# A hybrid decoder step: earlier splitting of the first merged sums, side work let out by chunk length, first x tile on another queue

## The chip, the core and the metric

The kernel runs on one core of a Trainium2 chip. A core has a matrix engine (TensorE, PE in the profile; its weight loads are shown as PEld), VectorE (DVE), ScalarE (ACT), GpSimd (POOL) and SyncE (SP), which work through their own instruction queues in order and wait for each other by semaphores. Data moves between the device memory and the core's memory (SBUF) by DMAs, which here are issued by SyncE and, at the end, by ScalarE. TensorE writes to eight PSUM banks. The metric is the device time of one execution, in microseconds; lower is better.

## The reference

One layer of a decoder trunk in float32, for 256 prompt tokens and 8 sample tokens (264 columns, N), model width 2048:

```
xn = rms_norm(x, g_mix);  z = xn @ w_in          # pool u | lru x | lru gelu gate | conv a | conv b
y_pool = pool_mixer(u) @ w_pool_br               # window means minus token, 4 groups, per-group map w_pool_grp
y_lru  = (rg_lru(causal_dwconv(lru_x)) * gelu(gate)) @ w_lru_br
y_conf = silu(layer_norm(causal_dwconv(a * sigmoid(b), 31 taps))) @ w_conf_br
gates  = sigmoid(xn @ w_gate + b_gate)           # three gates of width 2048
x = x + (g_a * y_pool + g_b * y_lru + g_c * y_conf) @ w_out
x = x + square(relu(rms_norm(x, g_mlp) @ w_up)) @ w_down      # inner width 8192
y = rms_norm(x, g_final)
```

The new states of the pooling, the two convolutions and the LRU are outputs too.

## The kernel before, in words

**Products in three parts.** A float32 product is made from three products of rounded parts: each operand is split into a high part (rounded to the matrix engine's fp32r format) and a low part (the rest). For each weight tile and k tile, `mm3` (L283) issues high x high, low weight x high input, high weight x low input, all through `mm` (L281), with a 128x128 weight tile and 264 columns.

**The weight stream.** All weights come as one list of chunks (`weight_plan`, L97). A dense chunk is two k tiles by 512 columns, so 2 x 4 x 3 = 24 matmuls. Four lru chunks and one grp chunk hold 128x128 blocks, 12 matmuls each, and one chunk, none, is empty and only keeps the pairs even. There are 472 dense chunks, 478 in all. Each pair is loaded to `raw` (6 chunks deep, `dma_pair`, L222) by SyncE. `split(j)` (L258) makes its high part in `whi` on ScalarE (L264) and its low part in `wlo` on VectorE (L265); both have four buffers, so chunk j can be split once TensorE has finished chunk j - 4.

Chunk numbers that matter, before the change: 0 to 15 are w_in for the lru x; 28 to 31 end w_in's pooling and first gelu-gate groups; 32 to 43 the second gelu-gate group with the lru chunks at 34, 37, 40 and 42; 44 to 59 the two conf groups of w_in; 60 to 69 the first gate group, with grp at 64 and none at 65; 86 starts the pooling branch projection, 87 the LRU branch projection; 182 to 189 are w_conf_br (group 0 ends at 184, 1 at 185, 2 at 188, 3 at 189); 190 starts w_out.

**The loop.** For chunk i the program writes, in this order: `split(i + 3)` (L1013), DMA issues, the chunk's matmuls, at a group's end the evacuation of its four PSUM tiles (mostly VectorE), and then `run_bg()` (L308), which lets out side work. The engines' queues hold the instructions in that order. There is no other scheduler: the place of an instruction in its engine's queue is set by the chunk in which it was written.

**Side work.** The branches between the projections (convolutions, LRU gates and scan, gelu, pooling, the conf branch) are lists of small operations in three queues, lru, pool and conf, in this order of preference. Each stage names an engine, a cost in microseconds, and how many chunks the next stage waits (`stage`, L296). Each engine has a credit; every `run_bg` adds an income (1.8 for ScalarE, 1.5 for VectorE, 2.4 for GpSimd; 1.3 and 1.0 once the flag lru is set), with at most half an income carried over, and lets out operations while the credit covers them. Work that is not queued is charged with `spend`. Other work is put off by a fixed number of chunks with `later` (L305). A flag such as pool, lru or conf (`mark`, L302) is set when all before it in the queue has been let out; the program asserts it before a chunk that reads the result. The pooling is: four running sums on GpSimd, four `diff` (L783, VectorE), a split in high and low parts (`stage_split`, L544), then `grp_mm` (L801) in the grp chunk, whose result is evacuated by ScalarE (L806) and split again. `lru_tail` (L568) holds tanh (L578), decay (L581, with another table), root, products and scan (L603) of the LRU. `lru_gate_mm` (L550) issues an lru chunk, its two sigmoids on ScalarE and, one chunk later, a product on VectorE (L562).

**The merged sums.** `branch_evac` (L840) multiplies a branch projection by its gate (L844). For the third branch it adds the partial sum of the other two on GpSimd (L850) and puts off the split for w_out: high part three chunks later on ScalarE (L856), low part five chunks later on VectorE (L860). The first w_out chunks, 190 to 193, read the four sums of group 0, chunk 194 on those of group 1.

**The start.** `dma_head` (L250) issues three loads on SyncE: norm weights with the first x tile and the first half weight chunk (396 KB), a second x tile with its half chunk, and the two other halves. Seventeen warm-up matmuls on constants (L376) come first on TensorE. The first x tile is made into its parts by VectorE (L394, L203), the first weights by ScalarE (L274).

Of the kernel before, what the change touches and what calls it, by code (L numbers as in the profile page):

```python
# [19 lines left out]
N = TP + TS  # L20
KD = D // P
# [35 lines left out]
HEAD = N + 512  # L57
FIRST = 16
CH = 1024
NRAW = 6  # L60
NHI = 4
LRU_AT = (1, 3, 5, 6)
GRP_AT = 3
WARM = 17
LEAD = 4
SINGLE = 16
# [30 lines left out]
def weight_plan():  # L97

    def gate(t):
        return ("w_gate", 0, 16, t)

    def w_in(m):
        return ("w_in", 0, 16, m)

    def branches(g):
        return [("w_pool_br", 0, 4, g), ("w_lru_br", 0, 8, g)]

    walks = [[w_in(1), w_in(2)], [w_in(0), w_in(3)], [w_in(4)], [w_in(6), w_in(5)], [gate(0)], [gate(4), gate(1)]]  # L110
    walks += [branches(0), [gate(5), gate(2)], branches(1), [gate(6), gate(3)], branches(2), [gate(7)], branches(3)]
    walks += [[gate(8 + g)] for g in range(4)]
    walks += [[("w_conf_br", 0, 4, g + i) for i in range(2)] for g in (0, 2)]
    walks += [[("w_out", 0, 16, m + i) for i in range(2)] for m in (0, 2)]
    for q in range(4):
        up = [("w_up", 0, 16, q * 4 + m) for m in range(4)]
        walks += [up[:2], up[2:]] if q else [up[:1], up[1:2], up[2:]]
        walks += [[("w_down", q * 16, 16, m + i) for i in range(2)] for m in (0, 2)]

    groups, chunks, at = [], [], 0  # L120
    for walk in walks:
        mine = range(len(groups), len(groups) + len(walk))
        groups += walk
        todo = {}
        for gi in mine:
            for c in range(groups[gi][2] // 2):
                todo.setdefault(slot_of(("dense", gi, c), groups), []).append((gi, c))
        places = sorted(todo, reverse=abs(max(todo) - at) < abs(min(todo) - at))
        order = []
        for place in places:  # L130
            todo[place].sort(key=lambda x: (x[1], x[0]) if mine[0] == 0 and place != places[-1] else x)
            order += todo[place]
        at = places[-1]
        for gi, c in order:
            own = [o for o in order if o[0] == gi]
            n = own.index((gi, c))
            chunks.append(("dense", gi, c, CH, n == 0, n == len(own) - 1))
            if groups[gi] == w_in(4) and n in LRU_AT:
                chunks.append(("lru", LRU_AT.index(n), 0, 512))
            if groups[gi] == gate(0) and n == GRP_AT:  # L140
                chunks += [("grp", 0, 0, 512), ("none", 0, 0, 0)]
    return groups, chunks
# [3 lines left out]
def hybrid_step(ctx: ExitStack, tc: tile.TileContext, first, par_in, st_in, wall, y_out, st_out):  # L146
    nc = tc.nc
# [4 lines left out]
    def f(ap):  # L152
        return ap.bitcast(F32)
# [26 lines left out]
    def both(t, slot, row, rows):  # L180
        out = []
        for r in (row, row + rows):
            at = SKEW + r * ROW + slot * OCT
            out.append(bass.AP(tensor=t.tensor, offset=t[:, at:].offset,
                               ap=[list(t.ap[0]), [HOP, N // (STRETCH * OCT)], [STEP, STRETCH], [1, OCT]]))
        return tuple(out)
# [4 lines left out]
    def in_sum(k):  # L191
        return both(a_all, 3 - k // 4, k % 4, 4)
# [4 lines left out]
    def v(t):  # L197
        return t.rearrange("p (a b c) -> p a b c", b=STRETCH, c=OCT)
# [17 lines left out]
    done = set()  # L216


    groups, chunks = weight_plan()
# [18 lines left out]
    head = [b_all[i] for i in (1, 2)]  # L238
# [9 lines left out]
        return head[0][:, KD + c * HEAD + N:KD + c * HEAD + HEAD]  # L248

    def dma_head():  # L250
        for t, a, b, o in ((0, 0, KD + HEAD, 0), (0, KD + HEAD, KD + 2 * HEAD, 0), (1, 0, CH, KD + 2 * HEAD)):
            nc.sync.dma_start(head[t][:, a:b], first[:, o + a:o + b])

    def dma_x(j):
# [31 lines left out]

    queues = {"lru": [], "pool": [], "conf": []}
    ready_at = dict.fromkeys(queues, 0)  # L290
    credit = {"act": 0.0, "dve": 0.0, "pool": 0.0}
    income = {"act": 1.8, "dve": 1.5, "pool": 2.4}
    now = [0]
# [11 lines left out]
    def later(n, fn):  # L305
        delayed.append((now[0] + n, fn))

    def run_bg():  # L308
        if "lru" in done:
            income.update(act=1.3, dve=1.0)  # L310
        for item in [d for d in delayed if d[0] <= now[0]]:
            delayed.remove(item)
            item[1]()
        for e in credit:
            credit[e] = min(credit[e], 0.5 * income[e]) + income[e]
        for q, todo in queues.items():
            while todo and ready_at[q] <= now[0]:
                if isinstance(todo[0], str):
                    if todo[0] not in done:
                        break  # L320
                    todo.pop(0)
                    continue
                eng, cost, fns, gap = todo[0]
                if eng != "none" and credit[eng] < min(cost, income[eng]):
                    break
                fns.pop(0)()
                if eng != "none":
                    credit[eng] -= cost
                if not fns:
                    todo.pop(0)  # L330
                    ready_at[q] = now[0] + gap

    def spend(**kw):
        for e, c in kw.items():
            credit[e] -= c
# [31 lines left out]


    dma_head()
    nc.vector.memset(ones, 1.0 / D)  # L370
    nc.vector.memset(eps, EPS)
# [446 lines left out]
    def gate_tile(br, g, m):  # L818
        if br == 2:
            return G[:, 4 * g + m, :]  # L820
        if br and g % 2:
            return GEL[:, m, :]
        return G[:, g % 2 * 8 + br * 4 + m, :]

    def partial(k):
        return (TM if k < 8 else RA)[:, k % 8, :]
# [13 lines left out]
    def branch_evac(br, g, m, ps):  # L840
        assert "grp" in done and (br < 1 or "lru" in done) and (br < 2 or "conf" in done)
        t = gate_tile(br, g, m)
        k = g * 4 + m
        nc.vector.tensor_tensor(t, ps[:, :N], t, op=ALU.mult)  # L844
        spend(dve=0.43)
        if br == 1:
            nc.gpsimd.tensor_tensor(partial(k), t, gate_tile(0, g, m), op=ALU.add)
            spend(pool=0.8)
        if br == 2:
            nc.gpsimd.tensor_tensor(t, t, partial(k), op=ALU.add)  # L850
            spend(pool=0.8)
            later_split(*in_sum(k), t, 3, 2)

    def later_split(hi, lo, x, n, gap):
        def one():
            nc.scalar.copy(hi, v(x))  # L856
            spend(act=0.4)

        def other():
            nc.vector.tensor_tensor(lo, v(x), f(hi), op=ALU.subtract)  # L860
            spend(dve=0.35)

        later(n, one)
        later(n + gap, other)
# [75 lines left out]
    def group(gi):  # L940
        name, k0, _, m = groups[gi]
        if name == "w_in":
            def rhs(i):
                return in_a(i)
            fn = {0: pool_evac, 1: lru_x_copy, 2: lambda c, p: lru_x_evac(4 + c, p), 3: gel_evac,
                  4: lambda c, p: gel_evac(4 + c, p), 5: ca_evac, 6: cb_evac}[m]
            return rhs, fn
        if name == "w_gate":
            return in_a, (lambda c, p: gate_evac(m // 4, m % 4, c, p))
        if name == "w_pool_br":  # L950
            assert "grp" in done
            return (lambda i: in_half(Q(), i)), (lambda c, p: branch_evac(0, m, c, p))
        if name == "w_lru_br":
            assert "lru" in done
            return (lambda i: in_half(LH(), i)), (lambda c, p: branch_evac(1, m, c, p))
        if name == "w_conf_br":
            assert "conf" in done
            return (lambda i: in_half(Q(), 4 + i)), (lambda c, p: branch_evac(2, m, c, p))
        if name == "w_out":
            return in_sum, (lambda c, p: out_evac(m * 4 + c, p))  # L960
        if name == "w_up":
            return bpart, (lambda c, p: up_evac(m // 4, (m % 4) * 4 + c, p))
        q = k0 // 16
        return (lambda i: hid(q, i)), (lambda c, p: down_evac(q, m * 4 + c, p))
# [43 lines left out]
    for i, ch in enumerate(chunks):  # L1008
# [69 lines left out]
        if i == 14:  # L1078
            later(0, x_rms)
        run_bg()  # L1080
    while delayed:
        now[0] += 1
        run_bg()
# [143 lines left out]
```

## Time and profile before

| what | value |
|---|---|
| median of 3 runs | 1314.7 us (1314.19 to 1316.95) |
| the profiled execution | 1315.07 us |
| its span in the trace | 1313.3 us |
| TensorE busy | 1300.7 us (99%) |
| VectorE busy | 839.9 us (64%) |
| ScalarE busy | 719.9 us (55%) |
| GpSimd busy | 98.3 us (7%) |
| bytes moved | 257.21 MB, mean 196 GB/s |

The profile shows one execution. Its own time is 1.8 us above its span, for what lies around the first and last instruction. A line of a timeline has the start and the length in microseconds, the engine, the line of the kernel, the operation, the tiles (written <- read), the shapes and the number of like instructions in a row; in square brackets stands how long the engine idled before it and what ended that. The kernel's helpers record many operations under one line, so that the tiles tell them apart. wlo and whi are the parts of the weights, A holds the parts of xn and later of the merged sums.

### The profile page before, as it was taken

How to read it: one execution, taken by the hardware profiler on the slowest of the kernel's cores; microseconds unless marked ns; L12 is line 12 of the kernel's file. 1: busy time of each engine (PE TensorE's matmuls, PEld its weight loads, DVE VectorE, ACT ScalarE, POOL GpSimd, SP SyncE). 2: the span in 40 equal slices, each digit the busy share in tenths (PEclk: the TensorE clock that was granted, in tenths of full speed). 3: DMA queues.
4: the chain of work that ended last, by engine and by line, in shares of the span. 5: the costliest groups of instructions: out<-in, count | busy, mean ns of one | idle time of the engine just before them, and what ended most of it. 6: DMA issues, size and time to landing. Idle time of an engine off the chain costs nothing.

```text
span 1313.3 us, 26597 instructions
## 1 busy us (share of the span) xinstructions
PE 1300.7 (99%) x11421; PEld 1298.1 (99%) x11421; DVE 839.9 (64%) x1126; ACT 719.9 (55%) x1034; POOL 98.3 (7%) x125
## 2 busy tenths in 40 slices
PE   9999999999999999999999999999999999999997
PEld 9999999999999999999999999999999999999996
DVE  8787898777776758577655554565446644564554
ACT  7667687676764645456545334553335533354454
POOL 0320020101012104012000000000000000000022
PEclk9999999999999999999999999999999999999998
DMA  9555556555565555555655555555555555555552
GB/s 347 210 185 186 184 200 218 195 192 196 194 224 194 189 197 184 198 193 169 218 193 193 194 193 193 195 194 192 194 194 194 194 196 194 194 198 194 194 196 77
DMA packets 40565, 257.21 MB, mean 196 GB/s; under 512 B 4480, under 2 KB 6528, under 8 KB 11520
## 3 DMA queue, kind: packets, MB, share of 16 engines
q1 hardware_dynamic: 40016, 254.92, 55.9%
q8 instruction: 89, 1.46, 0.4%
q10 hardware_dynamic: 432, 0.61, 0.1%
q14 instruction: 28, 0.23, 0.1%
HBM read 252.30 MB, written 3.21 MB: 195 GB/s over the span
## 4 chain that ended last, share of the span: by engine, by line
PE 97%; DVE 1%; ACT 1%; issue 0%; DVEq 0%; ACTq 0%
PE acc L281 97%; ACT whi L264 0%; DVE wlo L265 0%; PE acc L376 0%; DVE y L1115 0%; ACT tmp L578 0%; DVE tmp L628 0%; DVE G L844 0%; ACT L581 0%; DVE A L860 0%; ACT tmp L581 0%; DVE G L562 0%; DVE acc L1106 0%; DVEq L1204 0%; DVE G L1105 0%
## 5 line engine op out<-in xcount | busy, mean ns | idle before, releaser
L265 DVE TENSOR_TENSOR wlo<-raw,whi 128x1024 fp32r<-128x1024 f32 (+1 forms) x478 | 586.5, 1230 | 452.4 <-ACT whi L264 447.4
L264 ACT CAST whi<-raw 128x1024 fp32r<-128x1024 f32 (+1 forms) x478 | 493.6, 1036 | 534.4 <-PE acc L281 500.9
L281 PE MATMUL acc<-A,whi 128*128 128x264 f32 x3968 | 676.9, 274 | 2.0 <-DVE A L860 2.0
L281 PEld LDWEIGHTS acc<-A,whi 128*128 128x128 f32 x3968 | 597.1, 188 | 2.7 <-DVE A L860 2.2
L281 PE MATMUL acc<-A,wlo 128*128 128x264 f32 x1984 | 540.6, 274 | 0.3
L281 PEld LDWEIGHTS acc<-A,wlo 128*128 128x128 f32 x1984 | 370.1, 187 | 0.9 <-DVE wlo L265 0.9
L281 PE MATMUL acc<-xn,whi 128*128 128x264 f32 x2048 | 349.3, 274 | 0.0
L281 PEld LDWEIGHTS acc<-xn,whi 128*128 128x128 f32 x2048 | 308.3, 187 | 0.0
L281 PE MATMUL acc<-xn,wlo 128*128 128x264 f32 x1024 | 280.7, 274 | 0.0
L281 PEld LDWEIGHTS acc<-xn,wlo 128*128 128x128 f32 x1024 | 191.8, 187 | 0.0
L281 PE MATMUL acc<-Q,whi 128*128 128x264 f32 x776 | 139.3, 274 | 0.0
L281 PE MATMUL acc<-LH,whi 128*128 128x264 f32 x768 | 137.8, 274 | 0.0
L281 PEld LDWEIGHTS acc<-Q,whi 128*128 128x128 f32 x776 | 120.0, 187 | 0.0
L281 PEld LDWEIGHTS acc<-LH,whi 128*128 128x128 f32 x768 | 118.8, 187 | 0.0
L281 PE MATMUL acc<-Q,wlo 128*128 128x264 f32 x388 | 106.4, 274 | 0.0
L281 PE MATMUL acc<-LH,wlo 128*128 128x264 f32 x384 | 105.3, 274 | 0.0
L894 POOL TENSOR_TENSOR G<-G 128x264 f32<-128x264 f32 x28 | 26.2, 937 | 755.4 <-ACT G L892 754.1
L281 PEld LDWEIGHTS acc<-Q,wlo 128*128 128x128 f32 x388 | 72.7, 187 | 0.0
L281 PEld LDWEIGHTS acc<-LH,wlo 128*128 128x128 f32 x384 | 71.9, 187 | 0.0
L678 ACT ACTIVATE G<-tmp,par 128x256 f32<-128x256 f32 x120 | 54.4, 501 | 1.6 <-DVE G L681 1.5
L681 DVE TENSOR_TENSOR G<-G 128x1024 f32<-128x1024 f32 x30 | 36.6, 1219 | 0.0
L927 DVE TENSOR_TENSOR X<-X,acc 128x264 f32<-128x264 f32 x79 | 28.7, 423 | 4.9 <-PE acc L281 4.9
(173 smaller groups left out, 518.4 us busy)
## 6 DMA issues: line engine op xcount, KB each, us to landing
raw<-wall_dram SPq DMA_DIRECT2D x226, 1024.0 KB, 4.8
raw<-first_dram SPq DMA_DIRECT2D x14, 512.0 KB, 8.2
X<-first_dram SPq DMA_DIRECT2D x8, 264.0 KB, 8.2
raw<-wall_dram SPq DMA_DIRECT2D x4, 512.0 KB, 3.8
raw<-wall_dram SPq DMA_DIRECT2D x5, 256.0 KB, 3.3
y_dram<-y SPq DMA_DIRECT2D x3, 264.0 KB, 2.2
tmp<-st_dram SPq DMA_DIRECT2D x4, 188.0 KB, 5.1
so_dram<-tmp SPq DMA_DIRECT2D x4, 188.0 KB, 6.4
```

The costliest lines, as they stand in the source:

```text
L264: nc.scalar.copy(h, r)
L265: nc.vector.tensor_tensor(lo, r, f(h), op=ALU.subtract)
L281: nc.tensor.matmul(ps[:, :N], w[k == 1], x[k == 2], start=start, stop=stop)
L678: nc.scalar.activation(dst[:, ct, :TP], vext[:, ct, k:k + TP], AF.Copy, scale=par[:, w:w + 1])
L681: nc.vector.tensor_tensor(VC[:, :, :TP], VC[:, :, :TP], src[:, :, :TP], op=ALU.add)
L894: nc.gpsimd.tensor_tensor(sq2, sq2, t, op=ALU.add)
L927: nc.vector.tensor_tensor(X[:, m, :], X[:, m, :], ps[:, :N], op=ALU.add)
```

## The change

There are four edits, with the diff below.

- For group 0 of the third branch, the high part of a merged sum is made two chunks after its evacuation and the low part three after it, in place of three and five. Groups 1 to 3 stay.
- `run_bg` adds only half an income in an lru or grp chunk and none in the empty chunk. Between the flags xc and lru ScalarE's income is 1.6 in place of 1.8. The carried-over credit is unchanged.
- The queue of the pooling comes ahead of the queue of the LRU. The grp chunk and the empty one come two chunks earlier (62 and 63 in place of 64 and 65; the chunks up to 61 and from 66 on keep their numbers).
- The norm weights and the first x tile (280 of the 792 columns of the first load) are loaded by a DMA of their own on ScalarE's queue. SyncE's first load holds the other 512 columns, the first half weight chunk.

```
-GRP_AT = 3
+GRP_AT = 1
...
     def dma_head():
-        for t, a, b, o in ((0, 0, KD + HEAD, 0), (0, KD + HEAD, KD + 2 * HEAD, 0), (1, 0, CH, KD + 2 * HEAD)):
+        nc.scalar.dma_start(head[0][:, :KD + N], first[:, :KD + N])
+        for t, a, b, o in ((0, KD + N, KD + HEAD, 0), (0, KD + HEAD, KD + 2 * HEAD, 0), (1, 0, CH, KD + 2 * HEAD)):
             nc.sync.dma_start(head[t][:, a:b], first[:, o + a:o + b])
...
-    queues = {"lru": [], "pool": [], "conf": []}
+    queues = {"pool": [], "lru": [], "conf": []}
...
+    share = {"lru": 0.5, "grp": 0.5, "none": 0.0}
+
     def run_bg():
         if "lru" in done:
             income.update(act=1.3, dve=1.0)
+        elif "xc" in done:
+            income.update(act=1.6, dve=1.5)
+        part = share.get(chunks[min(now[0], len(chunks) - 1)][0], 1.0)
...
-            credit[e] = min(credit[e], 0.5 * income[e]) + income[e]
+            credit[e] = min(credit[e], 0.5 * income[e]) + part * income[e]
...
-            later_split(*in_sum(k), t, 3, 2)
+            later_split(*in_sum(k), t, *((3, 2) if g else (2, 1)))
```

## The prediction

> **What bounds the kernel now.** I read the page first, then the chain of work that ended last, the waits of TensorE's weight loads, and the timelines around each wait.
>
> ```profile
> PE 1300.7 (99%) x11421; PEld 1298.1 (99%) x11421; DVE 839.9 (64%) x1126; ACT 719.9 (55%) x1034; POOL 98.3 (7%) x125
> ```
>
> The page's first part: TensorE is busy for 99% of the 1313.3 us span, VectorE for 64%. A TensorE that is busy can still lose time between two matmuls, so the chain comes next (start, length, what):
>
> ```profile
> 0.78 3.79 PE acc L376 x17
> 4.61 42.21 PE acc L281 x360
> ...
> 621.43 680.66 PE acc L281 x6000
> ```
>
> The last 6000 matmuls of the stream take 680.66 us, 0.1134 us each. A dense chunk of 24 takes 2.72 us, an lru or grp chunk of 12 takes 1.36. The plan holds 472 x 24 + 5 x 12 = 11388 of them, 1291.9 us at that pace. They run from 4.61 to 621.43 + 680.66 = 1302.09, which is 1297.5 us. All that fewer waits could win there is the difference, 5.6 us. The 4.6 us ahead and the 11.2 us behind belong to the start and the final norm. Where the 5.6 us lie is shown by the waits of the weight loads (us in total, times, longest):
>
> ```profile
> PEld acc L281 <- DVE A L860: 2.2, 1, 2.2
> PEld acc L281 <- DVE wlo L265: 0.9, 3, 0.3
> ```
>
> One wait is for the low part of a merged sum, three are for low parts of weights. The rest is spread thinly, and the change doesn't touch it. What a wait costs is read from the starts of matmuls in TensorE's timeline, here at three of the four:
>
> ```profile
> 515.53 0.28 PE L281 MATMUL acc<-A,wlo 128*128 128x264 f32 x1
> 517.78 0.51 PE L281 MATMUL acc<-A,whi 128*128 128x264 f32 x2 [1.97 <-DVE A L860]
> 518.13 0.27 PE L281 MATMUL acc<-A,wlo 128*128 128x264 f32 x1
> ```
> ```profile
> 106.67 0.29 PE L281 MATMUL acc<-A,whi 128*128 128x264 f32 x1
> 107.10 0.39 PE L281 MATMUL acc<-A,wlo 128*128 128x264 f32 x1
> 107.32 0.39 PE L281 MATMUL acc<-A,whi 128*128 128x264 f32 x2
> ```
> ```profile
> 182.35 0.40 PE L281 MATMUL acc<-A,whi 128*128 128x264 f32 x2
> 182.74 0.39 PE L281 MATMUL acc<-A,wlo 128*128 128x264 f32 x1
> 182.97 0.40 PE L281 MATMUL acc<-A,whi 128*128 128x264 f32 x2
> ```
>
> From 515.53 to 518.13 are three steps: 2.60 us instead of 0.34, so 2.26 are lost. From 106.67 to 107.32 are two steps, 0.42 lost; from 182.35 to 182.97 three, 0.28 lost. The step after a wait is slow as well (0.22 from 107.10 to 107.32, against 0.11). The third wait for a weight is about as long as that of 106.67 (0.3 is the longest, and three make 0.9), so 0.4. Together 2.26 + 0.42 + 0.28 + 0.4 = 3.4 us. Counted in matmuls, the places are chunk 190 (the first of w_out), chunk 38, chunk 68, and chunk 48 for the one not shown.
>
> **First merged sums: split two chunks and three chunks behind.** VectorE, ScalarE and GpSimd ahead of chunk 190:
>
> ```profile
> 508.50 1.69 DVE L265 TENSOR_TENSOR wlo<-raw,whi 128x1024 fp32r<-128x1024 f32 x1 [1.43 <-ACT whi L264]
> 511.23 1.23 DVE L265 TENSOR_TENSOR wlo<-raw,whi 128x1024 fp32r<-128x1024 f32 x1 [1.03 <-ACT whi L264]
> 515.34 1.44 DVE L844 TENSOR_TENSOR G<-acc,G 128x264 f32<-128x264 f32 x4
> 516.71 3.71 DVE L860 TENSOR_TENSOR A<-G,A 128x264 fp32r<-128x264 f32 x4
> ```
> ```profile
> 508.38 1.35 ACT L856 CAST A<-G 128x264 fp32r<-128x264 f32 x4
> ```
> ```profile
> 502.04 8.77 POOL L850 TENSOR_TENSOR G<-G,tmp 128x264 f32<-128x264 f32 x8 [43.62 <-DVE G L844]
> ```
>
> The four low parts of group 0 (L860) stand in VectorE's order behind the evacuation of chunk 189 (L844), which needs that chunk's end. So the first is done at about 517.7, while chunk 190 wants it at 515.64. The change adds no instruction. It puts the high parts of group 0 into chunk 186, one chunk (2.72 us) ahead of the row of group 1 that ScalarE shows: 505.7 to 507.0, before its next cast can start. Their input, the first four of the eight GpSimd adds, is there at half of 8.77, 506.4; if ScalarE waits for it, 0.7 us, what is late is a cast of chunk 190, needed eight microseconds on. The low parts go into chunk 187, behind the split that ends at 510.19; no evacuation is queued there. They take about 1.45 us if they run as the four L844 do, or 3.71 beside the adds: done between 511.7 and 513.9, at least 1.7 early. Behind them stands the split of 511.23, then late by 0.4 to 2.7 us, done by 515.2 and wanted by chunk 191 at 518.2. The low parts of group 1 stay five chunks behind, due at chunk 194, about 526. Value: the whole 2.26; both ends of the unknown price lie under cover.
>
> **Side work by chunk length.** The credits of run_bg, carried from chunk to chunk on paper, say what moves. After chunk 33 VectorE holds 0.65. Chunk 34 (lru) adds 1.5 before, enough for two pooling differences of 0.8, and 0.75 after, enough for one. At chunk 42 (lru) ScalarE gets to 2.5 before (four tanh of 0.52) and to 1.2 after (two). Chunk 62 (grp) lets out the four high parts of the group map and one scan, chunk 63 (none) one low part. The flags come later: pool 38 instead of 37, b_term 60 instead of 55 (due 69), lru 85 instead of 79 (due 87), conf 176 instead of 170 (due 182). grp comes at 65 instead of 67. So the deferred work has at least two chunks, 5.4 us, of cover, and the conf branch has six chunks. No engine gets more to do; only the order moves. At the three waits:
>
> ```profile
> 104.78 0.40 DVE L788 SCALAR_TENSOR_TENSOR G<-qtmp 128x240 f32<-128x240 f32 x1
> 105.81 1.23 DVE L265 TENSOR_TENSOR wlo<-raw,whi 128x1024 fp32r<-128x1024 f32 x1
> 106.96 0.70 DVE L562 TENSOR_TENSOR G<-G,tmp 128x528 f32<-128x528 f32 x1
> ```
>
> *Chunk 38.* The second difference of chunk 34 begins at 104.78, and chunk 38's low part follows it, 1.03 us later. Without that difference ahead of it the low part runs from 104.78 to 106.0, and 106.78 is wanted: 0.42 won, 0.8 to spare. The product L562 and the difference then stand ahead of chunk 39's low part: 104.78 + 1.14 + 0.62 + 1.03 + 1.23 = 108.8, wanted at 109.5.
>
> ```profile
> 125.26 0.92 ACT L578 ACTIVATE tmp<-tmp,sp 128x264 f32<-128x264 f32 x2 [2.51 <-DVE G L562]
> 126.09 1.03 ACT L264 CAST whi<-raw 128x1024 fp32r<-128x1024 f32 x1
> 127.14 1.28 ACT L581 ACT_TABLE_LOAD   x1
> 129.66 1.03 ACT L264 CAST whi<-raw 128x1024 fp32r<-128x1024 f32 x1
> ```
>
> *Chunk 48.* ScalarE stands 2.51 us ahead of the last two tanh, which wait for VectorE. Then come a cast, the table load, three decays, and only at 129.66 chunk 48's cast. With the tanh let out two, three and three, the last two come behind that first cast, and table load and decays behind chunk 48's cast, which can start about when the two tanh end, near 126.2. That is 3.5 us sooner than now for a low part that was 0.3 late: 0.4 won, over 3 us to spare.
>
> ```profile
> 176.77 1.59 ACT L806 ACTIVATE G<-acc,par 128x264 f32<-128x264 f32 x4
> 178.24 2.26 ACT L638 ACTIVATE tmp<-tmp 128x528 f32<-128x528 f32 x4
> ```
>
> *Chunk 68.* It starts at 182.35 + 0.11, so the grp matmuls end two dense chunks ahead, at 177.0. L806 ends 1.35 behind that, and ScalarE does 2.26 us of gelu before chunk 68's cast. In the new order, with E for the end of grp, four Q casts follow L806 (1.35 like L856, to E + 2.7), then chunk 66's cast (1.03, E + 3.7) and its low part (1.23, E + 4.95), wanted at E + 5.55: 0.6 to spare. gelu begins six chunks after grp. 0.28 won. The three together: 1.1.
>
> **First x tile on ScalarE's queue.**
>
> ```profile
> 3.97 0.49 DVE L394 TENSOR_SCALAR A<-tmp 128x264 fp32r<-128x264 f32 x1 [2.71 <-DMA tmp<-first_dram]
> 0.74 1.33 SPq L252 DMA_DIRECT2D tmp<-first_dram  x3
> 0.73 1.28 ACT L373 ACT_TABLE_LOAD   x1 [0.73 <-PEq L1198]
> ```
> ```profile
> tmp<-first_dram SPq DMA_DIRECT2D x1, 396.0 KB, 3.2
> y_dram<-y ACTq DMA_DIRECT2D x1, 132.0 KB, 2.0
> ```
>
> ScalarE gains one issue of about 0.44 us (a third of 1.33). Behind it stands the table load, which would end at 2.5, not 2.0, ahead of the first weights near 4. SyncE keeps three issues. The 396 KB become 140 and 256. The tile could land 1.2 us sooner (2.0 for 132 KB, against 3.2). It buys nothing: the seventeen warm-up matmuls of the chain's first row hold TensorE until 4.57, and the first real one starts 0.04 later. Value 0, from -0.1 to +0.5 if the first weights come later beside the tile.
>
> **Sum.** 2.26 + 1.1 + 0 = 3.4 us off the profiled execution, 1315.07 to 1311.7. That execution lies 0.4 above the median of the runs shown, 1314.7; so the median becomes 1311.3. A measurement of this kernel can tell about 0.2%, 2.6 us, from no change.
>
> **Rivals.** *A new wait at chunk 64.* grp comes two chunks nearer to the crowded end of the conf projections:
>
> ```profile
> 168.44 3.94 POOL L689 TENSOR_TENSOR G<-tmp,par 128x248 f32<-128x248 f32 x4 [34.59 <-DVE tmp L665]
> 169.47 1.36 DVE L265 TENSOR_TENSOR wlo<-raw,whi 128x1024 fp32r<-128x1024 f32 x1
> ```
>
> Chunk 59 ends at 177.0 - 1.36 - 4 x 2.72 = 164.8, and VectorE finishes its evacuation, ahead of the split of 169.47, about 4.8 us behind that. If VectorE stays as late, two products (0.70 each, as L562) and chunk 64's low part (1.36) bring it to 7.6 behind, where 6.9 is wanted (two chunks, grp, one matmul). With the restart that is 0.8: 2.6 won, median 1312.1. Against it, two products and three scans that stand ahead of that evacuation now come behind it. For it, GpSimd's products run beside just these operations, where the split took 1.36 instead of 1.23. [...]
>
> *Pacing does nothing.* Low parts come as late at other chunks, and only the 2.26 remain: 1312.4, which is no change that can be measured.
>
> *The x tile comes late: slower.* If the DMA engines served SyncE's loads first, the tile would wait behind them:
>
> ```profile
> X<-first_dram SPq DMA_DIRECT2D x6, 264.0 KB, 8.6
> 5.60:14.00 8.40, 8.40 (x72) 8.40 (x71) 8.40 (x25) 7.47 (x15) 0.00 (x0) 1.00 1.02 400
> ```
>
> The X tiles of that stretch land 8.6 us behind their issue, under full load (DMA share 1.02, 400 GB/s). A first tile that lands at 0.7 + 8.6 puts the first real matmul at about 9.9, 5.3 late: net 1.9 slower, 1316.6. Behind all thirteen loads that are queued ahead of the chunk loop, 5.4 MB or 13.5 us, it is 10.2 late: net 6.8 slower, 1321.5. It decides from 3.4 us of lateness on. Against it, ScalarE's store at the end landed in 2.0 us.
>
> **How the numbers follow.** Forecast 0.66, a wait at chunk 64 or 66 0.2, pacing without effect 0.1, late tile 0.04. The forecast's own range is 1310.7 to 1312.0: the two lower runs shown are half a microsecond apart. The chunk-64 wait lies at 1312.1, the second rival at 1312.4, or 1313.2 with the tile's 0.5 and some spread. The range is 1310.6 to 1313.2 and leaves out the late tile. Faster by over 0.2% means under 1312.1: most of the first case and half of the second, 0.7. Same 0.26, slower 0.04.
>
> **What would show it.** The wait for L860 is gone from TensorE's waits, and the first four L860 stand between 510 and 514. No wait for a weight's low part is left at chunks 38, 48 and 68; one at chunks 64 to 66 would show the first rival. The first real matmul still starts near 4.6, however early the tile lands; a later start shows the third. The prediction is wrong if the matmul stretch, now 1297.5, isn't 3.0 to 3.6 us shorter.

## The result, and the profile after

The changed kernel takes 1311.5 us (median of 10 executions, 1311.29 to 1311.82). The kernel before takes 1314.6 us in the 10 executions beside it (1314.16 to 1317.05). The ratio is 0.9972, with a 95% interval of 0.9963 to 0.9982: faster, by 3.1 us.

The kernel before doesn't have one time but two: 50 of 94 executions beside the experiments lie around 1316.6 us and 44 around 1314.8, while those of the changed kernel lie within 0.6 us. The medians above are to be read with that; the last section shows by what their profiles differ.

In the profile after, the first part of the page has about the same busy times as before:

```profile
PE 1299.2 (99%) x11421; PEld 1297.5 (99%) x11421; DVE 841.0 (64%) x1126; ACT 720.6 (55%) x1034; POOL 102.5 (8%) x125
```

The chain that ended last, and the waits of the weight loads:

```profile
0.74 3.22 DMA tmp<-first_dram
...
3.98 0.72 ACT whi L275 x2
...
4.79 41.93 PE acc L282 x360
...
617.92 680.66 PE acc L282 x6000
```
```profile
PEld L382 <- issue: 0.7, 1, 0.7
PEld acc L282 <- ACT whi L275: 0.7, 1, 0.7
PEld acc L1098 <- DVE G L930: 0.4, 1, 0.4
```

The matmul stretch now runs from 4.79 to 617.92 + 680.66 = 1298.58, which is 1293.8 us, 3.7 less than the 1297.5 before. Neither of the two lines that carried the argument (the merged sums' low part, the weights' low parts) is left; the three waits that the view still lists are at the start and in the final norm. The first real matmul starts 0.18 us later, and the final norm takes 0.1 more. The span fell by 3.4 us, to 1309.9, and the profiled execution took 1311.82.

Three places in the timelines follow; chunk 38 comes in the account point by point. First, VectorE ahead of chunk 190, and TensorE at its start (start, length, engine, line, operation, tiles, shapes, count):

```profile
508.88 2.01 DVE L866 TENSOR_TENSOR A<-G,A 128x264 fp32r<-128x264 f32 x4
510.81 1.21 DVE L266 TENSOR_TENSOR wlo<-raw,whi 128x1024 fp32r<-128x1024 f32 x1
514.91 1.44 DVE L850 TENSOR_TENSOR G<-acc,G 128x264 f32<-128x264 f32 x4
```
```profile
514.18 0.28 PE L282 MATMUL acc<-A,whi 128*128 128x264 f32 x1
514.30 0.27 PE L282 MATMUL acc<-A,wlo 128*128 128x264 f32 x1
514.41 0.39 PE L282 MATMUL acc<-A,whi 128*128 128x264 f32 x2
```

The four low parts (L866, which was L860) are done at 510.89, ahead of the evacuation of chunk 189 (L850) in place of behind it. Chunk 190 starts at 514.18 and runs on without a gap. Then chunk 48, on ScalarE, and chunk 64, the place of the prediction's first rival, on VectorE and TensorE:

```profile
123.96 0.92 ACT L584 ACTIVATE tmp<-tmp,sp 128x264 f32<-128x264 f32 x2 [0.75 <-DVE G L568]
124.79 1.03 ACT L265 CAST whi<-raw 128x1024 fp32r<-128x1024 f32 x1
125.84 1.28 ACT L587 ACT_TABLE_LOAD   x1
```
```profile
166.12 1.93 DVE L606 TENSOR_TENSOR tmp<-tmp,G 128x528 f32<-128x528 f32 x2
168.00 1.66 DVE L266 TENSOR_TENSOR wlo<-raw,whi 128x1024 fp32r<-128x1024 f32 x1
```
```profile
170.76 0.27 PE L282 MATMUL acc<-A,wlo 128*128 128x264 f32 x1
```

Chunk 48's cast stands ahead of the table load, at 124.79, and not at 129.66 behind it. Chunk 64's low part is done at 169.66, and its first user starts at 170.76, with 1.1 us to spare: the rival's wait did not come.

### The profile page after: what moved, and what is told of

It is laid out like the page before. It is cut to its first block, busy times and chain, and to the rows that moved or that the text cites. A ratio compares the mean times of both kernels' runs of the same rounds, so it can differ in the third digit from the quotient of the medians.

```text
span 1309.9 us, 26606 instructions
## 1 busy us (share of the span) xinstructions
PE 1299.2 (99%) x11421; PEld 1297.5 (99%) x11421; DVE 841.0 (64%) x1126; ACT 720.6 (55%) x1034; POOL 102.5 (8%) x125
## 4 chain that ended last, share of the span: by engine, by line
PE 99%; DVE 0%; DMA 0%; ACT 0%; DVEq 0%; issue 0%
PE acc L282 99%; DMA tmp<-first_dram 0%; DVE y L1121 0%; ACT whi L275 0%; DVE acc L1112 0%; DVEq L1210 0%; DVE G L1111 0%; DVE acc L1110 0%; PE acc L1098 0%; PE acc L366 0%; ACT rstd L1105 0%; DVE G L930 0%; DVE X L929 0%; DVEq L1112 0%
```

## The experiments

Theory A is the prediction's own account: the earlier split of the merged sums is worth about 2.3 us, the pacing about 1.1, the x tile on the other queue nothing, and the parts add up. Its rivals give the gain to another part, or have one part take back what another gives; each expectation says by numbers what it would see. Eight kernels undo or do one part, or half of one. Two more bring the one wait to other lengths, and two look at the start. Ratios are to the kernel before, on the same chip.

### The merged sums alone

```
-            later_split(*in_sum(k), t, 3, 2)
+            later_split(*in_sum(k), t, *((3, 2) if g else (2, 1)))
```

> Before with the first edit alone (merged sums of group 0 split two and three chunks behind). Theory A, each wait has its own cause and the edits add up: the wait for the merged sum at chunk 190 goes, the three waits for a weight's low part stay, 2.2 to 2.3 us faster than before. Rival B, the 3.1 us are mostly a gain of the pacing, and chunk 190's wait only moves to a later chunk of w_out: 0 to 1 us faster, with a new wait between chunks 191 and 200.

Measured: 1312.35 us (1311.8 to 1312.66), ratio 0.9977 [0.9968, 0.9986]. All executions form one group, 2.5 us under the lower group of before (median 1314.86 on that chip, beside an upper one at 1316.55). The wait for L860 is gone, no new one follows it in TensorE's timeline, and the weights' waits stay:

```profile
PEld acc L281 <- DVE wlo L265: 0.8, 3, 0.3
```

This edit gives most of the gain, as A says, and it alone removes the second group.

### The pacing alone

GRP_AT, the queues' order, the shares and the income of 1.6 as in the change; merged sums and loads as before.

```
-GRP_AT = 3
+GRP_AT = 1
...
-    queues = {"lru": [], "pool": [], "conf": []}
+    queues = {"pool": [], "lru": [], "conf": []}
...
+    share = {"lru": 0.5, "grp": 0.5, "none": 0.0}
...
+        elif "xc" in done:
+            income.update(act=1.6, dve=1.5)
+        part = share.get(chunks[min(now[0], len(chunks) - 1)][0], 1.0)
...
-            credit[e] = min(credit[e], 0.5 * income[e]) + income[e]
+            credit[e] = min(credit[e], 0.5 * income[e]) + part * income[e]
```

> Before with the pacing edits alone (half income in lru and grp chunks, none in the empty one, 1.6 for ScalarE, pooling first, grp two chunks earlier). Theory A: the three waits at chunks 38, 48 and 68 go, that of chunk 190 stays at 2.2, 1.0 to 1.2 us faster. Rival B, waits come back near chunks 64 to 66 in its place: 0.3 us faster or less, with a wait for a weight's low part left.

Measured: 1314.04 us (1313.13 to 1315.96), ratio 0.9991 [0.9982, 0.9999]. Two groups again: six executions around 1313.7, five around 1315.5. Lower group against lower group it is 1.1 us faster, which is A's 1.1. The waits for weights are gone from the profile, the one for the merged sum stays:

```profile
PEld acc L281 <- DVE A L865: 2.2, 1, 2.2
```

The medians of all executions can't show this part, since each depends on how many of few executions fell into which group.

### The x tile's load alone

```
-        for t, a, b, o in ((0, 0, KD + HEAD, 0), (0, KD + HEAD, KD + 2 * HEAD, 0), (1, 0, CH, KD + 2 * HEAD)):
+        nc.scalar.dma_start(head[0][:, :KD + N], first[:, :KD + N])
+        for t, a, b, o in ((0, KD + N, KD + HEAD, 0), (0, KD + HEAD, KD + 2 * HEAD, 0), (1, 0, CH, KD + 2 * HEAD)):
```

> Before with the first x tile on ScalarE's queue alone. Theory A: it moves nothing that ends later, within 0.2 us of before, all four waits as before. In the profile after the change the first real matmul starts 0.18 us later, but the first four chunks run at 0.113 us a matmul and not at 0.120. Rival C, the edit costs: 0.2 us slower, with the slow spacing of 0.120 back. Rival D, the edit gives the faster spacing: 0.1 to 0.3 us faster, spacing 0.113 in chunks 1 to 3.

Measured: 1315.28 us (1314.38 to 1317.23), ratio 1.0002 [0.9993, 1.0011]; lower group at 1314.88, as before's 1314.86. The tile lands 3.4 us after its issue, and the first real matmul starts at 4.78:

```profile
tmp<-first_dram ACTq DMA_DIRECT2D x1, 140.0 KB, 3.4
```

This part does nothing, as the prediction had it, though not for its reason (see the two experiments on the start).

### The change without the x tile's load

The merged sums and the pacing as in the change, the loads as before.

> The changed kernel without the edit of the first load. Theory A: as fast as the changed kernel within 0.2 us, so 2.9 to 3.3 us faster than before, and the first real matmul at 4.6. Rival C, that edit costs: 3.3 to 3.6 us faster than before. Rival D, that edit gave the spacing of the first chunks: 2.7 to 2.9 us faster, spacing 0.120 in chunks 1 to 3.

Measured: 1311.68 us (1311.25 to 1311.93), ratio 0.9972 [0.996, 0.9983], the changed kernel's own time. The parts alone sum to 2.5 + 1.1 + 0 = 3.6, against a measured 3.2 (1314.86 - 1311.68). One group is itself up to 0.9 us wide, so the 0.4 between doesn't show that one part takes from another, and it doesn't rule out a few tenths. The first real matmul starts at 4.74 here, later than the expected 4.6 though the loads are as before.

### Half an income in the lru chunks, and nothing else of the pacing

```
+    share = {"lru": 0.5}
...
+        part = share.get(chunks[min(now[0], len(chunks) - 1)][0], 1.0)
...
-            credit[e] = min(credit[e], 0.5 * income[e]) + income[e]
+            credit[e] = min(credit[e], 0.5 * income[e]) + part * income[e]
```

> Before with half an income in the lru chunks alone (income, grp, queue order and merged sums as before). Theory A: chunk 34 lets out one pooling difference and chunk 42 three tanh, so the waits at chunks 38 and 48 go (0.8 us), while those of chunk 68 (0.3) and chunk 190 (2.2) stay. Rival B, the waits come from the incomes and the grp place together: all three weight waits stay.

Measured: 1315.66 us (1314.0 to 1315.89), ratio 0.9999 [0.999, 1.0008]; the lower group lies at 1314.05, 0.8 us under before's 1314.88. Six of the ten executions fell into the upper group, which hides the 0.8 in the ratio. The waits of chunks 38 and 48 are gone; that of chunk 68 stays:

```profile
PEld acc L281 <- DVE wlo L265: 0.2, 1, 0.2
```

The 0.8 us are the prediction's 0.42 + 0.4. The half income in the grp chunk and the none in the empty one were not tried alone.

### The grp chunk two chunks earlier, pooling first, no pacing

```
-GRP_AT = 3
+GRP_AT = 1
...
-    queues = {"lru": [], "pool": [], "conf": []}
+    queues = {"pool": [], "lru": [], "conf": []}
```

> Before with grp two chunks earlier and the pooling queue first, and nothing else (full income in lru, grp and empty chunks). Theory A: the waits at chunks 38 and 48 stay, that of chunk 68 shrinks or goes, and a new one stands at chunk 64, because VectorE comes late out of the conf evacuation: 0.5 to 1.2 us there, so 0.2 to 1 us slower than before. Rival B: moving grp alone is free, no wait at chunks 64 to 66, 0.3 us faster.

Measured: 1315.19 us (1314.53 to 1316.94), ratio 1.0002 [0.9992, 1.0011]; lower group at 1315.13 against before's 1314.88. The wait of chunk 68 is gone, those of chunks 38 and 48 stay, and a new one stands at chunk 64, shown here on TensorE and VectorE:

```profile
171.81 0.29 PE L281 MATMUL acc<-A,whi 128*128 128x264 f32 x1
172.48 0.39 PE L281 MATMUL acc<-A,wlo 128*128 128x264 f32 x1 [0.38 <-DVE wlo L265]
```
```profile
169.18 0.81 DVE L603 TENSOR_TENSOR_SCAN tmp<-tmp,tmp 128x256 f32<-128x256 f32 x1
171.07 1.35 DVE L265 TENSOR_TENSOR wlo<-raw,whi 128x1024 fp32r<-128x1024 f32 x1 [1.07 <-ACT whi L264]
```

From 171.81 to 172.48 one step takes 0.67 us, and by the spacing of the steps behind it 0.6 to 0.7 are lost in all. So the first rival's wait is real in this kernel, at the place and nearly at the price (0.8) that the prediction gave; the shares and the income of 1.6, which the full change has beside it, keep it away. Which of the two does was not separated. VectorE's conf evacuation came about as late as the rival had it (it ends at 169.28, 4.3 us behind chunk 59). The last link was another: ScalarE's four activations that wait for this evacuation (L673, 168.02 to 170.10) stood ahead of its cast (L264), and VectorE was idle for 1.07 us until that came; it was not held up by its own products.

### The low parts as late as before, the high parts two chunks behind

```
-            later_split(*in_sum(k), t, 3, 2)
+            later_split(*in_sum(k), t, *((3, 2) if g else (2, 3)))
```

> Before with the high parts of group 0 two chunks behind, low parts still five behind. Theory A, the place of the low parts in VectorE's queue is the cause: the wait of 2.2 us at chunk 190 stays, no gain. [...] Rival B, the high parts were late: the wait shrinks to under 1 us.

Measured: 1315.18 us (1314.7 to 1316.9), ratio 0.9999 [0.9991, 1.0008], in two groups (1314.78 and 1316.72, with before's at 1314.88 and 1316.68). ScalarE makes the high parts at 505.67, and the wait stays:

```profile
505.67 1.35 ACT L856 CAST A<-G 128x264 fp32r<-128x264 f32 x4
```
```profile
PEld acc L281 <- DVE A L860: 2.2, 1, 2.2
```

The high parts were not what came late. The profile is of the upper group (1316.76 us): in the 3.4 us from 519.20 to 522.60, behind the wait, its granted clock is 0.50.

### The low parts one chunk earlier only, the high parts as before

```
-            later_split(*in_sum(k), t, 3, 2)
+            later_split(*in_sum(k), t, *((3, 2) if g else (3, 1)))
```

> Before with the high parts of group 0 three chunks behind as before and the low parts four behind, in chunk 188 instead of 189. Theory A: they no longer stand behind the evacuation of chunk 189, the wait at chunk 190 goes, 2.2 us off the lower group of before, and there is no upper group any more (all executions within 1 us). Rival B, the low parts run too slowly beside GpSimd's adds and need all the lead of the change: a wait of 0.5 to 1.5 us stays.

Measured: 1312.68 us (1311.97 to 1313.06), ratio 0.9976 [0.9967, 0.9985], one group, 1.1 us wide and 2.2 us under before's lower one.

```profile
513.33 3.04 DVE L860 TENSOR_TENSOR A<-G,A 128x264 fp32r<-128x264 f32 x4
```

The low parts run from 513.33 to 516.37. Chunk 190 starts at 515.01, and the wait is gone all the same: the first of the four is done at 514.23 and the second at 515.12, 1.3 us ahead of its use in the second half of the chunk. So it is enough that the low parts stand one chunk further ahead in VectorE's queue, in front of the next split and the last evacuation. This is the cause as the prediction named it.

### The first sum early, the other fifteen as before

```
-            later_split(*in_sum(k), t, 3, 2)
+            later_split(*in_sum(k), t, *((3, 2) if k else (2, 1)))
```

> Before, with only the first of the four merged sums of group 0 split early (two and three chunks behind), the other three as before. The wait should move half a chunk on, to the second k tile of chunk 190, and last 0.7 us instead of 2.0. [...] Rival, the halved clock has nothing to do with the length of the wait: two groups 1.7 us apart as before.

Measured: 1312.93 us (1312.39 to 1313.22), ratio 0.9978 [0.9969, 0.9987], one group, 1.8 us under before's lower one (1314.72). A wait is left, for the second sum, half a chunk on:

```profile
516.71 0.28 PE L281 MATMUL acc<-A,wlo 128*128 128x264 f32 x1
517.00 0.49 PE L281 MATMUL acc<-A,whi 128*128 128x264 f32 x2
```
```profile
PEld acc L281 <- DVE A L860: 0.2, 1, 0.2
```

One step takes 0.29 us here, and the waits' row says 0.2; about 0.3 us are lost in all, where a wait of 0.7 was expected. With so short a wait the second group is gone, in 11 executions.

### The low parts one chunk later still

```
-            later_split(*in_sum(k), t, 3, 2)
+            later_split(*in_sum(k), t, *((3, 2) if g else (3, 3)))
```

In this kernel chunk 190 is written ahead of its sums' low parts and so reads old contents in their place; the wait falls on chunk 191.

> Before with the low parts of group 0 six chunks behind (chunk 190 instead of 189). The wait at chunk 190 should last 3.0 to 3.4 us instead of 2.0. [...] Rival, the halved clock has nothing to do with the length of the wait: half of the executions in the upper group as before.

Measured: 1317.02 us (1315.26 to 1318.72), ratio 1.001 [1.0001, 1.0019]. Nine of eleven executions lie in an upper group from 1316.99 on, two at 1315.26 and 1315.63.

```profile
517.77 0.28 PE L281 MATMUL acc<-A,wlo 128*128 128x264 f32 x1
520.79 0.49 PE L281 MATMUL acc<-A,whi 128*128 128x264 f32 x2 [2.74 <-DVE A L860]
```

The wait grew from 1.97 to 2.74 us, a little less than the expected step. The upper group grew from about half to nine of eleven, where the rival has half.

### The other half of the first load on ScalarE's queue

```
-        for t, a, b, o in ((0, 0, KD + HEAD, 0), (0, KD + HEAD, KD + 2 * HEAD, 0), (1, 0, CH, KD + 2 * HEAD)):
+        nc.scalar.dma_start(head[0][:, KD + N:KD + HEAD], first[:, KD + N:KD + HEAD])
+        for t, a, b, o in ((0, 0, KD + N, 0), (0, KD + HEAD, KD + 2 * HEAD, 0), (1, 0, CH, KD + 2 * HEAD)):
```

> Before with the first load in two, the other way round: the first x tile as SyncE's first load, the first half weight chunk (256 KB) on ScalarE's queue. Theory A, a small load lands no sooner here and ScalarE's queue is a little slower at the start: the tile lands 3.1 to 3.3 us after its issue, the weights 3.4 or more, first real matmul at 4.7 to 5.0, time as before within 0.3 us. Rival, ScalarE's queue is as fast as SyncE's and the tile was late because SyncE's loads are served first: now the tile lands under 3.0 and the first matmul starts under 4.6.

Measured: 1314.95 us (1314.73 to 1317.0), ratio 0.9998 [0.9988, 1.0007]. From the DMA part of its page (queue, size, us from issue to landing):

```profile
tmp<-first_dram ACTq DMA_DIRECT2D x1, 256.0 KB, 3.5
tmp<-first_dram SPq DMA_DIRECT2D x1, 140.0 KB, 3.3
```

The first real matmul starts at 4.74. On either queue the small load (140 KB) lands no sooner than the 396 KB did: 3.3 us after its issue here and 3.4 on ScalarE's queue, against 3.2 before.

### Fourteen warm-up matmuls

```
-WARM = 17
+WARM = 14
```

> Before with 14 warm-up matmuls instead of 17. The prediction said that the warm-up holds TensorE until 4.57 us, so that an earlier x tile buys nothing; by that the first real matmul would now start near 4.0 to 4.2. Theory A, it is the data (the tile lands at 3.9 to 4.0, then 0.5 for its high part) that holds the first matmul: it starts at 4.5 to 4.7 as before, and the time is as before within 0.3 us.

Measured: 1315.94 us (1314.79 to 1316.59), ratio 1.0001 [0.9992, 1.001]. TensorE and VectorE at the start:

```profile
0.78 3.15 PE L376 MATMUL acc<-const-bfloat16-1.0 128*128 128x256 bf16 x14 [0.78 <-PEq L1198]
4.67 0.56 PE L281 MATMUL acc<-A,whi 128*128 128x264 f32 x1 [0.74 <-DVE A L394]
```
```profile
4.03 0.49 DVE L394 TENSOR_SCALAR A<-tmp 128x264 fp32r<-128x264 f32 x1 [2.77 <-DMA tmp<-first_dram]
```

The warm-ups end at 3.93, 0.6 us sooner, and the first real matmul comes at 4.67 (4.61 before): TensorE idles for 0.74 us and waits for VectorE, which waits for the tile. So the data sets the start, and the warm-ups fill the time until then.

The time is not as before within 0.3 us, though the ratio of the medians hides it: six of the ten executions lie from 1315.69 to 1316.04, between the two groups of before, and one (1314.79) in the lower group. The profile is of one of the six (1315.78) and has no slow stretch behind its wait for the merged sum: the 910 matmuls from 518.48 on take 103.53 us, as in the profile of before. The last section comes back to it.

## Why the prediction was right, point by point

**The number.** Predicted were 1311.3 us, with 1310.6 to 1313.2; measured were 1311.5.

**The budget.** The four waits were to give back 3.4 us, with the matmul stretch 3.0 to 3.6 shorter. It is 3.7 shorter, just outside the band that the prediction had set for itself. The first 360 matmuls took 41.93 us and not 42.21, and no edit was shown to cause those 0.28. By the starts of matmuls 24 to 96 the profile of before shows 0.120 us a step, that of after 0.113. Without the 0.28 the stretch is 3.4 shorter. The rest of the 5.6 us is not spread as thinly as the prediction had it: the first 96 matmuls of the profile of before take 12.07 us, 1.2 more than the steady pace gives. The time fell from 1315.07 to 1311.82, 3.25 us, as the first matmul came 0.18 later and the norm and what lies around the span took 0.25 more.

**The merged sums.** Predicted 2.26; alone 2.5 in the lower groups, 2.2 with only the low parts moved. The mechanism (behind the evacuation of chunk 189 in VectorE's queue) is shown by the pair of kernels that move only the high and only the low parts. The low parts took 2.01 us, between the bounds of 1.45 and 3.71. They stand from 508.88 to 510.89 and not between 510 and 514, as chunk 190 itself comes 1.2 us sooner. The split behind them was done at 512.02 (predicted by 515.2 at the latest).

**The pacing.** Predicted 1.1; alone 1.1 in the lower groups, 0.8 of it from the lru chunks' half income. So the second rival, that the pacing does nothing, falls. At chunk 38 the low part follows without the difference ahead of it, which now comes behind it, in VectorE's timeline of after:

```profile
104.68 1.22 DVE L266 TENSOR_TENSOR wlo<-raw,whi 128x1024 fp32r<-128x1024 f32 x1
106.44 0.40 DVE L794 SCALAR_TENSOR_TENSOR G<-qtmp 128x240 f32<-128x240 f32 x1
```

At chunk 48 the cast came 4.9 us sooner, not 3.5, since the two tanh ahead of it began 1.3 us sooner than before (123.96 and not 125.26), where the prediction had left them in place. Chunk 66's low part was done at 175.47, 0.7 us ahead of its first user (0.6 predicted), since the chunk starts at 176.09 and wants it one step on.

**The x tile.** Value 0 was right by luck, as its reason was wrong. The step that failed is "the tile could land 1.2 us sooner": it was taken from a store at the end of the kernel (132 KB in 2.0 us), while a load of 140 KB at the start took 3.3 to 3.4 us, against 3.2 for 396 KB. The other half, that the warm-up matmuls hold TensorE, failed too: fourteen of them leave the first real one where it was. The late tile, the third rival, didn't come.

**The first rival.** A wait at chunk 64 had 0.2. It doesn't come in the full change, and comes without the shares and the income of 1.6, at 0.6 to 0.7 us. In the profile after, VectorE's two products and the split run beside GpSimd's work (165.08 to 169.80) and are slower: the products took 1.93 us and not 1.40, and the split 1.66 and not 1.23, 0.96 us in all and more than the 0.13 (1.36 and not 1.23) that the row of before showed. GpSimd's work is slower there as well: of its four products the first, ahead of them, took 0.67 us and the last, beside them, 1.13. What holds the two engines up was not shown. The cover lasted, as the conf evacuation ends 2.4 us behind chunk 59 and not 4.8.

**What it missed.** The kernel before has two times, and the longest wait decides between them. The prediction saw one profile of the lower group, and the spread of the three runs shown (1314.19 and 1316.95) went unread. Against the lower group the changed kernel wins 2.8 us (1314.32, seven of the ten executions beside it; the kernel without the x tile's load won 3.2 against its own lower group), where the forecast was 3.4. So 1311.3 and 1311.5 agree better than the gains do: the forecast started from 1314.7, 0.4 above that lower group. Where half of the executions lie 1.8 us higher, the change wins some 0.9 more on average. The prediction put no number to that.

None of the other kernels is faster than the changed one; the one without the x tile's load has the same time.

## What to carry to other kernels

When a matrix engine is 99% busy, count its matmuls, take their steady pace, and look for the few steps that take longer: here each was traced to an instruction that stood too far back in another engine's queue, and the cure was its place, not its cost. When work is let out by a budget per chunk, check whether it follows the chunk's length: here the short chunks, with a full budget, made what followed them late. And when the runs of a kernel fall in two groups, compare group with group, and profile both.

## What the runs showed of the hardware

**A wait of 2 us can cost 4.** The profile of the pacing alone is of its upper group (1315.96 us). TensorE's timeline behind the wait for the merged sum:

```profile
516.93 0.51 PE L281 MATMUL acc<-A,whi 128*128 128x264 f32 x2 [1.97 <-DVE A L865]
517.62 0.27 PE L281 MATMUL acc<-A,wlo 128*128 128x264 f32 x1
517.74 0.60 PE L281 MATMUL acc<-A,whi 128*128 128x264 f32 x2
518.13 0.42 PE L281 MATMUL acc<-A,wlo 128*128 128x264 f32 x1
```

The same stretch by windows (window, its length, busy time and instructions of PE, PEld, DVE, ACT, POOL, then the granted clock, the DMA share, GB/s), first of this kernel, then of the kernel before, whose profile is of its lower group:

```profile
514.90:517.70 2.80, 0.83 (x7) 0.77 (x7) 2.80 (x7) 0.91 (x1) 2.80 (x5) 1.00 0.31 132
517.70:521.20 3.50, 3.50 (x18) 3.50 (x17) 3.50 (x6) 0.00 (x0) 1.57 (x2) 0.51 0.00 0
521.20:524.00 2.80, 2.80 (x26) 2.80 (x26) 2.10 (x4) 2.31 (x5) 0.00 (x0) 1.00 0.83 263
```
```profile
517.70:521.20 3.50, 3.42 (x30) 3.42 (x31) 3.50 (x5) 0.61 (x1) 2.42 (x3) 1.00 0.00 0
```

Behind the wait the granted clock is 0.51 over the 3.50 us from 517.70 to 521.20, and a step takes 0.22 us (518.13 to 518.35) and not 0.113: 18 matmuls where the same stretch holds 30 otherwise. By the 0.51 the clock is halved for about 3.4 us, which as an estimate loses 1.7 us on top of the 2.26, about the distance of the two groups (1.7 to 1.9). The slow steps begin behind the end of the wait, at about 517.8, where the wait ended at 516.93.

Other profiles agree with the groups of their times:

| kernel | profiled execution | behind the wait |
|---|---|---|
| the high parts two chunks behind | 1316.76 us | clock 0.50 from 519.20 to 522.60 |
| the low parts one chunk later still | 1317.00 us | clock 0.50 from 521.20 to 524.60, where the wait ended at 520.79 |
| the other half of the first load on ScalarE's queue | 1317.00 us | the next 910 matmuls take 105.19 us |
| before | 1315.07 us | clock 1.00 from 517.70 to 521.20; the next 910 matmuls take 103.53 us |
| the first sum early | 1312.93 us | clock 1.00 from 514.90 to 524.60 |

The first three are of upper groups. Over 94 executions of the kernel before, the mean granted clock is 0.9976 in the lower group and 0.9967 in the upper.

How often it falls goes with the length of the wait: 9 of 11 at 2.74 us, 50 of 94 at 1.97, 0 of 11 at some 0.3, by the groups of the times. With the same wait of 1.97 us the clock fell in the profile of the pacing alone and not in that of before. What decides it in one execution, and from which length of a wait on, was not shown.

**The start has its own scatter.** The first real matmuls are slow, for a different time in each profile. In that of before the second to the fourth step take 0.22 us each, and from 5.63 on a step takes 0.12; in that of after the steps take 0.22 us until 6.47. In the profile with fourteen warm-up matmuls the first 360 take 42.93 us, 0.72 longer than in that of before (42.21), and start 0.06 later, so they end 0.8 us later. That is most of the 1.0 us by which this execution lies above the lower group, and six of the ten lie there. Whether fewer warm-ups are the cause isn't shown by one profile.

The second source is SyncE's third load (512 KB, the next weights). In the profiles of before and after it landed 4.8 and 4.6 us after its issue, and in six others 5.6 to 6.4 us after it. In that of the other half on ScalarE's queue it landed at 7.76 (1.64 + 6.12), ScalarE's cast of these weights began at 7.78, and TensorE's 25th matmul came at 8.45 (8.03 in that of before). TensorE's weight loads wait twice for the high parts of the first weights in eight profiles, 0.8 to 1.4 us in all, and once in four, 0.4 to 0.7 us; before (0.5) and after (0.7) are among the four. So the starts of two profiles can differ by nearly as much as the pacing is worth.
